# Encoder trunk: the first loads in another order, the first norms between the projections, the keys normed together

## The chip, the cores and the metric

The kernel runs on one core of a Trainium2 chip. The metric is the time of one execution on the device, in microseconds (us). Three runs of the kernel before took 3086.29, 3086.44 and 3088.57 us, median 3086.44.

## The reference, cut to what matters

The reference is an encoder trunk of two layers on 512 tokens of width 1024. What bears on the change is its beginning and the projection of the keys and values:

```python
h = layer_norm(x, ln_in_g, ln_in_b)
for l in range(DEPTH):
    proj = h @ w_in[l]
    qa, ka, va, qb, kb, vb = jnp.split(proj, SPLITS, axis=-1)
    ...
    qa = apply_axial_rope(rms_norm(qa, qn_g[l]), cos, sin)
    ka = apply_axial_rope(rms_norm(ka, kn_g[l]), cos, sin)
    oa = global_attention(qa, ka, va)
    ob = window_sink_attention(qb, kb, vb, sink[l], slopes)
    ...
```

`layer_norm` subtracts the mean of a row, divides by its standard deviation and applies a gain and a bias. `rms_norm` divides each head of 64 numbers by its root mean square. `apply_axial_rope` rotates the halves of each head by tables of cosines and sines. Behind that come attention, an output projection, another layer norm, a product-key expert layer (PEER) and a third layer norm; the change doesn't touch them.

## The kernel before, in words

The 512 tokens are four chunks of 128 rows. The tile `h` holds them with the tokens on the partitions. A float32 product is made exact enough by splitting both factors into a rounded part and a rest (`hi`, `lo`), both in a shorter matmul format, and adding three products.

The head of the kernel goes as follows.

1. SP, whose queue issues the loads, loads chunk 0 of `x` into `h` (line 144), the gain and the bias of the first layer norm (each as a copy on all 128 partitions, line 97), the chunks 1 to 3 of `x`, the identity matrix for transposes on TensorE (`ident`, line 149), and then small tables: `iota4`, `look`, `cos`, `sin`, `dist`, the gains `gq` and `gk`, `sk`, `gn`.
2. In each layer `load_split` (line 208) loads 1 MB of `w_in` into a ring of four tiles (`ws`, tag `wst`, line 138) and makes the rounded part on ScalarE (ACT, line 216) and the rest on VectorE (DVE, line 217). The first two are `w_k` and `w_v`, the keys and values of both head groups. Four of `w_q` follow.
3. A loop over the chunks 0, 1, 2, 3 (line 237) norms the chunk (layer 0 only, `layer_norm`, lines 106 to 120), transposes it by eight TensorE transposes (`transpose_rows`, line 129, with a cast on ACT in line 134 and the rest on DVE in line 136), and then multiplies it with `w_k` and with `w_v` (`proj`, lines 227 to 229, 24 matmuls each). The keys of global attention are normed and rotated at once, chunk by chunk (`norm_rope`, lines 183 to 198).
4. Then come the four blocks of `w_q` with all chunks (line 264). In the second of these the queries are normed and rotated by `norm_rope`, in the third and fourth the keys are transposed (`flip_k`).

A layer norm takes on DVE two `bn_stats` (line 110), one `bn_aggr` (line 103), an inverse square root by eleven small instructions, each of which needs the one before (`rsqrt`, lines 87 to 92), and two passes over 1024 columns (lines 114 and 116). `norm_rope` takes a square on ACT (line 188), a sum on DVE (line 189), the same `rsqrt`, three multiplications and two additions (lines 191 to 198).

The order on each engine is not the order of the source. A planner goes through the instructions with costs of its own and gives an engine the first in the source that is ready by its reckoning; the hardware then keeps that order on each engine. Tiles of one tag are a ring of so many buffers. `rsqrt` has rings of two (`rs_a`, `rs_t`) and four (`rs_y`), in which the inverse roots of the layer norms and of the key norms stand one behind the other in the order of the source.

Of the kernel before, what the change touches and what calls it, by code (L numbers as in the profile page):

```python
# [18 lines left out]
P = 128  # L19
# [26 lines left out]
def encoder_kernel(ctx: ExitStack, tc: tile.TileContext, x, ln_in_g, ln_in_b, w_in, qn_g, kn_g, sink,  # L46
# [48 lines left out]
    def bload(src, n, tag):  # L95
        t = sm.tile([P, n], F32, tag=tag, name=tag, bufs=1)
        nc.sync.dma_start(t, src[None, :].to_broadcast([P, n]))
        return t
# [41 lines left out]
        nc.sync.dma_start(t, src)  # L140
        return t

    for c in range(NC):
        nc.sync.dma_start(h[:, c, :], x[c * P:(c + 1) * P, :])
        if c == 0:
            g_in = bload(ln_in_g, D, "ln_g")
            b_in = bload(ln_in_b, D, "ln_b")
    ident = cp.tile([P, P], F32, name="ident")
    nc.sync.dma_start(ident, ident_c)
    iota4 = ws.tile([P, 2048], F32, tag="wst", name="iota4").bitcast(F16)[:, :P * 4]  # L150
    nc.sync.dma_start(iota4, iota4_c)
    iota2 = cp.tile([P, P, 2], F16, name="iota2")
# [9 lines left out]
    for l in range(L):  # L162
# [14 lines left out]
        def rotary_tables(g_t):  # L177
            for fn, src in (("c", cos), ("s", sin)):
                t = pj.tile([P, NC, HD], F32, tag="tab" + fn, name="tab" + fn, bufs=1)
                pool.tensor_tensor(out=t, in0=src, in1=bc(g_t[:, None, :], [P, NC, HD]), op=MUL)  # L180
                tabs[fn] = t

        def norm_rope(src, n, c, dst):

            nr = pj.tile([P, 3, 8, HD], F32, tag="nr", name="nr", bufs=1)
            sq, xn, t2 = (nr[:, i, :n, :] for i in range(3))
            ms = sm.tile([P, 8], F32, tag="nr_ms", name="nr_ms")[:, :n]
            act.activation(sq, src, AF.Square)
            v.tensor_reduce(out=ms, in_=sq, axis=AX.X, op=ADD)
            r = rsqrt(ms, 1.0 / HD, RMS_EPS, n, "nr")  # L190
            v.tensor_tensor(out=xn, in0=src, in1=bc(r[:, :, None], [P, n, HD]), op=MUL)
            v.tensor_tensor(out=t2, in0=xn, in1=bc(tabs["s"][:, c:c + 1, :], [P, n, HD]), op=MUL)
            v.tensor_tensor(out=xn, in0=xn, in1=bc(tabs["c"][:, c:c + 1, :], [P, n, HD]), op=MUL)
            xr = xn.rearrange("p n (a f) -> p (n a) f", a=2)
            tr = t2.rearrange("p n (a f) -> p (n a) f", a=2)
            dr_ = dst.rearrange("p n (a f) -> p (n a) f", a=2)
            v.tensor_tensor(out=dr_[:, :, :16], in0=xr[:, :, :16], in1=tr[:, :, 16:], op=ADD)
            v.tensor_tensor(out=dr_[:, :, 16:], in0=xr[:, :, 16:], in1=tr[:, :, :16], op=ADD)
# [6 lines left out]
        pj = sbuf(f"pj{l}", bufs=2)  # L205
        hTh = pj.tile([P, KD, S], F32R, name="hTh", bufs=1)
        hTl = pj.tile([P, KD, S], F32R, name="hTl", bufs=1)
        def load_split(src, nm):

            w = load_w(src, nm)  # L210
            r = []
            for i in range(2):
                x_ = w[:, i * D:(i + 1) * D]
# [16 lines left out]
            return b  # L230

        rotary_tables(gk)
        krs = {}
        if l == 0:
            layer_norm(gat[0], g_in, b_in)
        wk = load_split(w_in[l, 0], "w_k")
        for c in gat + dense:
            if l == 0 and c != gat[0]:
                layer_norm(c, g_in, b_in)
            cs = slice(c * P, (c + 1) * P)  # L240
            transpose_rows(h[:, c, :], hTh[:, :, cs], f"tr_h{c}", lo=hTl[:, :, cs])
            if c == gat[0]:
                wv = load_split(w_in[l, 1], "w_v")
            b = proj(c, wk, "ps_k")
            krs[c] = kr = pj.tile([P, 4, HD], F32, tag="kr", name="kr", bufs=NC)
            act.copy(kr.rearrange("p a d -> p (a d)"), b[:, :256])
            norm_rope(kr[:, 0:2, :], 2, c, kr[:, 0:2, :])
            b = proj(c, wv, "ps_v")
            act.copy(vN[:, c, :], b[:, :256])

        def flip_k(c):
            kh = pj.tile([P, 4, 2, HD], F32R, tag="kh", name="kh", bufs=1)
            kl = pj.tile([P, 4, 2, HD], F32R, tag="kl", name="kl", bufs=1)
            kx = bc(krs[c][:, :, None, :], [P, 4, 2, HD])
            act.copy(kh, kx)
            v.tensor_tensor(out=kl, in0=kx, in1=kh.bitcast(F32), op=SUB)
            for src, dst in ((kh, khh), (kl, kll)):
# [840 lines left out]
```

## Time and profile before

| what | value |
|---|---|
| time of the profiled execution | 3086.3 us |
| its span | 3084.5 us |
| lowest, median, highest of three runs | 3086.29, 3086.44, 3088.57 us |
| TensorE matmul (PE) busy | 2989.5 us, 97% of the span, 17858 instructions |
| TensorE weight load (PEld) busy | 2704.7 us, 88% |
| VectorE (DVE) busy | 2453.0 us, 80% |
| ScalarE (ACT) busy | 1311.1 us, 43% |
| GpSimd (POOL) busy | 748.8 us, 24% |
| granted TensorE clock, mean | 0.993 of full speed |

The busy time of an engine is the time in which it ran an instruction; idle time is told by what ended it. The first of forty equal slices of the span has PE at six tenths, all others but the second layer's beginning at eight or nine tenths. A granted clock of 1.00 is 2.4 GHz, 0.50 is 1.2 GHz; a stretch with a value between had both.

### The profile page before, as it was taken

What the parts mean: (1) busy time and instruction counts of PE and PEld (TensorE: products, weight loads), DVE (VectorE), ACT (ScalarE), POOL (GpSimd) and SP (SyncE); (2) the same over time, 40 slices, a digit from 0 to 9 for tenths busy, and PEclk for the clock granted to TensorE, in tenths of its full rate; (3) what the DMA queues carried; (4) which work ended last, traced back from release to release, by engine and by line L of the source; (5) the groups of instructions that cost most, each with busy time, mean ns of one, the idle gap of its engine ahead of it and who ended that gap; (6) DMA issues with size and microseconds to landing.
All of it is one profiled execution on the core that took longest, in us unless ns stands there. A gap on an engine that the chain in (4) does not pass through costs nothing. (4 is left out here: it accounts for less than half of the span.)

```text
span 3084.5 us, 47606 instructions
## 1 busy us (share of the span) xinstructions
PE 2989.5 (97%) x17858; PEld 2704.7 (88%) x17858; DVE 2453.0 (80%) x5207; ACT 1311.1 (43%) x2586; POOL 748.8 (24%) x524
## 2 busy tenths in 40 slices
PE   6999899999999999999999999999999999999998
PEld 6989887899999999999888888779999999999997
DVE  6777999678777777877777779987787787787777
ACT  2664268343333333333347532773433333333332
POOL 0000000014444444444000000000244344444540
PEclk9999999999999999999999999999999999999999
DMA  4113567659888888888520236675698988888882
GB/s 178 42 56 129 212 232 287 219 199 333 317 322 313 320 318 313 320 317 314 189 96 15 71 132 244 245 290 179 246 334 305 325 315 313 322 317 311 324 311 92
DMA packets 262232, 749.46 MB, mean 243 GB/s; under 512 B 19952, under 2 KB 130288, under 8 KB 231792
## 3 DMA queue, kind: packets, MB, share of 16 engines
q1 hardware_dynamic: 188272, 477.94, 42.8%
q0 software_dynamic: 73728, 268.47, 24.1%
q8 instruction: 140, 2.29, 0.3%
q14 instruction: 92, 0.75, 0.1%
HBM read 691.81 MB, written 54.53 MB: 242 GB/s over the span
## 5 line engine op out<-in xcount | busy, mean ns | idle before, releaser
L921 POOL DMA_INDIRECT gt<-in_dram,idx x512 | 742.3, 1450 | 2062.7 <-DVE idx L912 1197.7
L779 PE MATMUL ps_a<-xTh,uh 128*128 128x384 f32 x1824 | 610.6, 335 | 3.7 <-ACT uh L776 3.7
L781 PE MATMUL ps_a<-xTh,ul 128*128 128x384 f32 x1824 | 612.2, 336 | 0.0
L780 PE MATMUL ps_a<-xTl,uh 128*128 128x384 f32 x1824 | 610.8, 335 | 0.0
L966 PE MATMUL ff<-vh,wl 128*128 128x512 f32 x1476 | 576.4, 391 | 0.0
L964 PE MATMUL ff<-vh,wh 128*128 128x512 f32 x1476 | 574.9, 389 | 0.0
L965 PE MATMUL ff<-vl,wh 128*128 128x512 f32 x1476 | 574.5, 389 | 0.0
L997 ACT CAST vh<-vt 128x1024 fp32r<-128x1024 f32 x246 | 258.5, 1052 | 607.8 <-PE ff L966 308.1
L998 DVE TENSOR_TENSOR vl<-vt,vh 128x1024 fp32r<-128x1024 f32 x246 | 301.2, 1224 | 195.8 <-ACT vh L997 194.7
L779 PEld LDWEIGHTS ps_a<-xTh,uh 128*128 128x128 f32 x1824 | 342.7, 188 | 14.4 <-ACT uh L776 5.6
L780 PEld LDWEIGHTS ps_a<-xTl,uh 128*128 128x128 f32 x1824 | 342.6, 188 | 10.4
L927 DVE CUSTOM_DVE_ANT_0 junk<-gt,h 128x1024 bf16<-128x1024 f32 x256 | 313.1, 1223 | 37.6 <-DMA gt<-in_dram,idx 33.0
L781 PEld LDWEIGHTS ps_a<-xTh,ul 128*128 128x128 f32 x1824 | 342.5, 188 | 0.1
L1004 ACT CAST wh<-w 128x384 fp32r<-128x384 f32 x246 | 126.3, 513 | 478.3 <-DVE w L1001 474.3
L938 DVE SCALAR_TENSOR_TENSOR gacc<-gt,gw,gacc 128x1024 f32<-128x1024 f32 x252 | 311.6, 1280 | 21.3 <-DMA gt<-in_dram,idx 21.3
L966 PEld LDWEIGHTS ff<-vh,wl 128*128 128x128 f32 x1476 | 277.2, 188 | 57.6
L964 PEld LDWEIGHTS ff<-vh,wh 128*128 128x128 f32 x1476 | 277.0, 188 | 49.6 <-ACT wh L1004 0.9
L965 PEld LDWEIGHTS ff<-vl,wh 128*128 128x128 f32 x1476 | 277.2, 188 | 48.6
L777 DVE TENSOR_TENSOR ul<-ut,uh 128x1024 fp32r<-128x1024 f32 x228 | 277.9, 1219 | 21.7 <-ACT uh L776 21.7
L776 ACT CAST uh<-ut 128x1024 fp32r<-128x1024 f32 x228 | 239.7, 1052 | 121.8 <-PE ps_a L780 120.5
L1005 DVE TENSOR_TENSOR wl<-w,wh 128x384 fp32r<-128x384 f32 x246 | 137.5, 559 | 158.9 <-ACT wh L1004 158.9
L772 PE MATMUL ps_a<-xTd,ut 128*128 128x384 f32 x448 | 156.1, 493 | 0.0
(261 smaller groups left out, 4857.4 us busy)
## 6 DMA issues: line engine op xcount, KB each, us to landing
ut<-in_dram SPq DMA_DIRECT2D x128, 1024.0 KB, 8.4
vt<-in_dram SPq DMA_DIRECT2D x128, 1024.0 KB, 7.2
w_pq<-in_dram SPq DMA_DIRECT2D x48, 1024.0 KB, 5.0
gg<-G SPq DMA_DIRECT2D x62, 768.0 KB, 13.8
G<-stg SPq DMA_DIRECT2D x24, 1920.0 KB, 7.0
w_o<-in_dram SPq DMA_DIRECT2D x24, 1024.0 KB, 4.8
w_q<-in_dram SPq DMA_DIRECT2D x8, 1024.0 KB, 6.3
gt<-in_dram,idx POOLq DMA_INDIRECT x512, 7.3
```

Source lines behind the costliest of these rows:

```text
L777: v.tensor_tensor(out=ul.rearrange(ff), in0=us, in1=uh.rearrange(ff).bitcast(F32), op=SUB)
L779: pe.matmul(b[:, :ND], uh[:, k, :], xTh[:, k, :], start=k == 0, stop=False)
L780: pe.matmul(b[:, :ND], uh[:, k, :], xTl[:, k, :], start=False, stop=False)
L781: pe.matmul(b[:, :ND], ul[:, k, :], xTh[:, k, :], start=False, stop=k == KD - 1)
L921: pool.indirect_dma_start(out=t, out_offset=None, in_=src, in_offset=bass.IndirectOffsetOnAxis(ap=idx[:, j:j + 1], axis=0))
L927: v.tensor_tensor_reduce(out=jk, in0=t, in1=h[:, c, :], op0=MUL, op1=ADD, scale=1.0, scalar=0.0, accum_out=a_[:, j:j + 1])
L938: v.scalar_tensor_tensor(acc[j % 2], t, w_[:, j:j + 1], acc[j % 2], op0=MUL, op1=ADD)
L964: pe.matmul(b, wh[:, cs], vh[:, ns], start=blk == 0, stop=False)
L965: pe.matmul(b, wh[:, cs], vl[:, ns], start=False, stop=False)
L966: pe.matmul(b, wl[:, cs], vh[:, ns], start=False, stop=blk == NB - 1)
L997: act.copy(vh, vt[:, bi, :])
L998: v.tensor_tensor(out=vl, in0=vt[:, bi, :], in1=vh.bitcast(F32), op=SUB)
```

## The change

The loads come in another order: chunk 0 of `x`, gain, bias, `ident`, chunk 1, `w_k`, chunk 2, `w_v`, chunk 3, and only then the tables. `w_k` and `w_v` of layer 0 are loaded there and handed to `load_split`, so that nothing else is loaded for them later.

Chunk 0 is normed as before. The chunks 1 to 3 have a norm of their own, `first_norm`: ACT sums the row (a copy with a sum), DVE makes the mean and its negative from it by two small instructions, ACT sums the squares of the row less its mean, and DVE does `rsqrt` and the two passes. What ACT writes beside the sums goes into a tile of the ring `wst`. The norm of chunk c+1 stands in the source between the transposes of chunk c and its projections.

`w_k` is split behind the transposes of chunk 0, in both layers. The keys of the four chunks lie in one tile; in the loop only their squares and sums are left, and `norm_keys` does one `rsqrt` over 8 columns, three multiplications over 512 columns and eight additions for all four chunks behind the loop, in both layers.

```diff
-    for c in range(NC):
+    def load_x(c):
         nc.sync.dma_start(h[:, c, :], x[c * P:(c + 1) * P, :])
-        if c == 0:
-            g_in = bload(ln_in_g, D, "ln_g")
-            b_in = bload(ln_in_b, D, "ln_b")
+
+    load_x(0)
+    g_in = bload(ln_in_g, D, "ln_g")
+    b_in = bload(ln_in_b, D, "ln_b")
     ident = cp.tile([P, P], F32, name="ident")
     nc.sync.dma_start(ident, ident_c)
+    load_x(1)
+    w_first = [load_w(w_in[0, 0], "w_k")]
+    load_x(2)
+    w_first.append(load_w(w_in[0, 1], "w_v"))
+    load_x(3)
+
+    def first_norm(c):
+
+        hc = h[:, c, :]
+        jk = ws.tile([P, 2048], F32, tag="wst", name="sq")[:, :D]
+        s1 = sm.tile([P, 2], F32, tag="fn_s", name="fn_s")
+        mean = sm.tile([P, 2], F32, tag="fn_m", name="fn_m")
+        act.activation(jk, hc, AF.Copy, accum_out=s1[:, 0:1])
+        v.tensor_scalar(mean[:, 0:1], s1[:, 0:1], -1.0 / D, None, op0=MUL)
+        v.tensor_scalar(mean[:, 1:2], s1[:, 0:1], 1.0 / D, None, op0=MUL)
+        act.activation(jk, hc, AF.Square, bias=mean[:, 0:1], accum_out=s1[:, 1:2])
+        r = rsqrt(s1[:, 1:2], 1.0 / D, LN_EPS, 1, "fnr")
+        v.scalar_tensor_tensor(hc, hc, mean[:, 1:2], g_in, op0=SUB, op1=MUL)
+        v.scalar_tensor_tensor(hc, hc, r, b_in, op0=MUL, op1=ADD)
+
+    layer_norm(0, g_in, b_in)
...
+        def norm_keys(kr, ms):
+
+            nr = pj.tile([P, 3, 8, HD], F32, tag="nr", name="nr", bufs=1)
+            xn, t2 = (nr[:, i].rearrange("p (c n) d -> p c n d", c=NC) for i in (1, 2))
+            s4 = [P, NC, 2, HD]
+            r = rsqrt(ms.rearrange("p c n -> p (c n)"), 1.0 / HD, RMS_EPS, NC * 2, "nk").rearrange("p (c n) -> p c n", n=2)
+            v.tensor_tensor(out=xn, in0=kr[:, :, 0:2, :], in1=bc(r[:, :, :, None], s4), op=MUL)
+            v.tensor_tensor(out=t2, in0=xn, in1=bc(tabs["s"][:, :, None, :], s4), op=MUL)
+            v.tensor_tensor(out=xn, in0=xn, in1=bc(tabs["c"][:, :, None, :], s4), op=MUL)
+            for c in range(NC):
+                xr, tr, dr_ = (t[:, c, 0:2, :].rearrange("p n (a f) -> p (n a) f", a=2) for t in (xn, t2, kr))
+                v.tensor_tensor(out=dr_[:, :, :16], in0=xr[:, :, :16], in1=tr[:, :, 16:], op=ADD)
+                v.tensor_tensor(out=dr_[:, :, 16:], in0=xr[:, :, 16:], in1=tr[:, :, :16], op=ADD)
...
-        def load_split(src, nm):
-
-            w = load_w(src, nm)
+        def load_split(src, nm, w=None):
+
+            w = load_w(src, nm) if w is None else w
...
         rotary_tables(gk)
-        krs = {}
-        if l == 0:
-            layer_norm(gat[0], g_in, b_in)
-        wk = load_split(w_in[l, 0], "w_k")
+        kr = pj.tile([P, NC, 4, HD], F32, tag="kr", name="kr", bufs=1)
+        kms = sm.tile([P, NC, 2], F32, tag="k_ms", name="k_ms", bufs=1)
+        wk = wv = None
         for c in gat + dense:
-            if l == 0 and c != gat[0]:
-                layer_norm(c, g_in, b_in)
             cs = slice(c * P, (c + 1) * P)
             transpose_rows(h[:, c, :], hTh[:, :, cs], f"tr_h{c}", lo=hTl[:, :, cs])
             if c == gat[0]:
-                wv = load_split(w_in[l, 1], "w_v")
+                wk = load_split(w_in[l, 0], "w_k", w_first[0] if l == 0 else None)
+            if l == 0 and c != dense[-1]:
+                first_norm(c + 1)
+            if c == gat[0]:
+                wv = load_split(w_in[l, 1], "w_v", w_first[1] if l == 0 else None)
             b = proj(c, wk, "ps_k")
-            krs[c] = kr = pj.tile([P, 4, HD], F32, tag="kr", name="kr", bufs=NC)
-            act.copy(kr.rearrange("p a d -> p (a d)"), b[:, :256])
-            norm_rope(kr[:, 0:2, :], 2, c, kr[:, 0:2, :])
+            act.copy(kr[:, c].rearrange("p a d -> p (a d)"), b[:, :256])
+            sq = pj.tile([P, 3, 8, HD], F32, tag="nr", name="nr", bufs=1)[:, 0, :2, :]
+            act.activation(sq, kr[:, c, 0:2, :], AF.Square)
+            v.tensor_reduce(out=kms[:, c, :], in_=sq, axis=AX.X, op=ADD)
             b = proj(c, wv, "ps_v")
             act.copy(vN[:, c, :], b[:, :256])
+        norm_keys(kr, kms)
```

## Rows read from the trace of the kernel before

**Rows 1.** The view by stretches: for each stretch (us) its length, the busy time of each engine with its instructions, the granted clock, the share and the rate of the DMA engines.

```profile
0.00:60.00 60.00, 31.86 (x203) 29.72 (x204) 38.32 (x131) 14.58 (x24) 2.13 (x6) 0.94 0.52 192
60.00:280.00 220.00, 210.41 (x1656) 201.22 (x1656) 162.59 (x461) 126.46 (x434) 1.48 (x2) 0.99 0.20 72
```

**Rows 2.** The view of waits, TensorE matmuls alone, the first 62 us: who waited for whom, us in total, times, longest.

```profile
PE tr_h L129 <- DVE ln_mv L103: 12.5, 1, 12.5
PE tr_h L129 <- DVE h L116: 7.5, 3, 3.1
PE ps_k L227 <- ACT whi L216: 7.2, 1, 7.2
PE ps_k L228 <- DVE wlo L217: 0.7, 1, 0.7
```

**Rows 3.** The timeline of SP, which issues the loads: start (us), time of the issue, load.

```profile
0.75 0.39 SPq L144 DMA_DIRECT2D h<-in_dram  x1
...
3.86 0.45 SPq L149 DMA_DIRECT2D ident<-in_dram  x1
...
7.87 0.33 SPq L160 DMA_DIRECT2D sin<-in_dram  x1
9.64 0.33 SPq L161 DMA_DIRECT2D dist<-in_dram  x1
...
12.21 0.33 SPq L97 DMA_DIRECT2D gk<-in_dram  x1
...
14.09 0.50 SPq L140 DMA_DIRECT2D w_k<-in_dram  x1
...
15.11 11.75 SPq L140 DMA_DIRECT2D w_q<-in_dram  x4
```

**Rows 4.** The view of DMA issues, first 20 us: load, count, KB each, median us from issue to landing.

```profile
w_k<-in_dram SPq DMA_DIRECT2D x1, 1024.0 KB, 6.5
...
ident<-in_dram SPq DMA_DIRECT2D x1, 64.0 KB, 8.5
...
gq<-in_dram SPq DMA_DIRECT2D x1, 32.0 KB, 3.2
```

**Rows 5.** The view of waits of SP, up to 140 us: who waited for whom, us in total, times, longest.

```profile
SPq L161 <- DMA h<-in_dram: 1.4, 1, 1.4
```

**Rows 6.** The timeline of VectorE: start (us), duration, line, operation.

```profile
7.59 0.16 DVE L90 SCALAR_TENSOR_TENSOR lnrt<-lnry 128x1 f32<-128x1 f32 x1
...
9.34 1.28 DVE L116 SCALAR_TENSOR_TENSOR h<-h,lnry,ln_b 128x1024 f32<-128x1024 f32 x1
...
12.33 0.19 DVE L103 BATCH_NORM_AGGREGATE ln_mv<-ln_st 128x2 f32<-128x12 f32 x1
...
28.84 0.17 DVE L87 TENSOR_SCALAR nra<-nr_ms 128x2 f32<-128x2 f32 x1
28.92 0.15 DVE L87 TENSOR_SCALAR lnra<-ln_mv 128x1 f32<-128x1 f32 x1
...
32.39 1.28 DVE L116 SCALAR_TENSOR_TENSOR h<-h,lnry,ln_b 128x1024 f32<-128x1024 f32 x1
```

**Rows 7.** The timeline of TensorE matmuls: start (us), duration, line, operation, and in brackets the idle time before it and what ended it.

```profile
21.67 0.58 PE L227 MATMUL ps_k<-whi,hTh 128*128 128x256 f32 x1 [7.21 <-ACT whi L216]
...
33.73 1.92 PE L129 MATMUL tr_h<-ident,h 128*128 128x128 f32 x8 [3.12 <-DVE h L116]
...
62.46 0.28 PE L229 MATMUL ps_v<-whi,hTl 128*128 128x256 f32 x1
```

**Rows 8.** The view by stretches (columns as in the first group), one for each chunk: from its first projection (chunk 0) or its first transpose (chunks 1 to 3) to its last projection.

```profile
21.67:30.61 8.94, 8.26 (x48) 7.76 (x48) 6.76 (x13) 3.58 (x5) 0.00 (x0) 1.00 1.01 426
33.73:42.26 8.53, 8.52 (x56) 8.10 (x56) 4.01 (x23) 1.85 (x4) 0.00 (x0) 0.80 0.13 43
44.44:52.03 7.59, 7.35 (x56) 6.72 (x56) 4.50 (x24) 2.27 (x5) 0.00 (x0) 1.00 0.00 0
54.21:62.47 8.26, 8.26 (x56) 8.04 (x57) 4.39 (x8) 4.55 (x7) 0.00 (x0) 0.79 0.17 65
```

**Rows 9.** The view by lines, shapes apart, first 100 us (the row of L363 from the whole span): line, engine, operation, tiles and shapes, count, busy us, mean ns of one, idle us before and its releasers.

```profile
L136 DVE TENSOR_TENSOR hTl<-tr_h,hTh 128x512 fp32r<-128x512 f32 x8 | 5.3, 688 | 2.5 <-ACT hTh L134 2.5
L110 DVE BATCH_NORM_STATS2 ln_st<-h 128x6 f32<-128x512 f32 x8 | 5.1, 673 | 4.6 <-DMA h<-in_dram 4.6
...
L191 DVE TENSOR_TENSOR nr<-q,nry 128x512 f32<-128x512 f32 x3 | 2.1, 692 | 0.1
...
L198 DVE TENSOR_TENSOR kr<-nr 128x64 f32<-128x64 f32 x4 | 1.4, 358 | 0.0
...
L134 ACT CAST hTh<-tr_h 128x512 fp32r<-128x512 f32 x8 | 4.6, 586 | 21.6 <-PE tr_h L129 21.6
...
L216 ACT CAST whi<-w_k 128x1024 fp32r<-128x1024 f32 x2 | 2.0, 1042 | 5.5 <-DMA w_k<-in_dram 5.5
...
L363 ACT ACTIVATION_READ_ACCUMULATOR osq<-ps_o 128x1 f32 x128 | 26.8, 209 | 0.0
```

**Rows 10.** The view of waits, TensorE matmuls alone, from 1530 to 1590 us, the same loop in layer 1.

```profile
PE ps_k L229 <- DVE hTl L136: 2.8, 3, 1.9
PE ps_k L228 <- DVE wlo L217: 1.0, 1, 1.0
PE ps_k L227 <- ACT hTh L134: 1.0, 3, 0.4
```

More of the change, by code (lines that the diff above doesn't have):

```diff
@@ L253, in flip_k @@
             kl = pj.tile([P, 4, 2, HD], F32R, tag="kl", name="kl", bufs=1)
-            kx = bc(krs[c][:, :, None, :], [P, 4, 2, HD])
+            kx = bc(kr[:, c, :, None, :], [P, 4, 2, HD])
             act.copy(kh, kx)
```

## The prediction

> **What bounds the kernel now.** I read the busy shares first, then the slices and the stretches, then TensorE's waits in the stretch that stands out. TensorE is busy for 2989.5 of 3084.5 us, so only its 95 us of idle time and its stretches at the lower clock can be won. The slices put the largest hole at the start: in the first 60 us TensorE is busy for 31.86 us, 28.1 us idle, while the next 220 us hold 9.6 us of idle time [rows 1]. The change works in that hole. Its waits name three causes: 12.5 us until the first transpose, 7.2 us until the first key projection, and 7.5 us in three pieces before the transposes of chunks 1 to 3 [rows 2].
>
> First piece. Chunk 0 is normed at 9.34 + 1.28 = 10.62 us [rows 6], yet the transposes start at 12.5. The releaser named there had long been done; what landed then is `ident`, issued at 3.86 and 8.5 us on its way, that is 12.36 us [rows 3, 4], behind three chunks of `x`.
>
> Second piece. `w_k` is issued only at 14.09 and lands 6.5 us later at 20.6 [rows 3, 4]; the cast follows, and the first projection runs at 21.67 [rows 7].
>
> Third piece. The mean of chunk 1 is ready on VectorE at 12.33, but its inverse root begins at 28.92, directly behind the first instruction of the key root of chunk 0 at 28.84 [rows 6]. The rings of `rsqrt` are handed out in the order of the source, in which that key root stands first, and it needs the finished key projection. So each norm ends behind the projections of the chunk before (chunk 1: 32.39 + 1.28 = 33.67), and TensorE, which stops at 30.61, waits [rows 7, 8].
>
> From 54.21 on TensorE is dense, and the first query projection follows the last value projection at 62.46 without a gap [rows 7, 8]. That moment is my mark: what it moves forward should move the end forward, since all behind it is counted from compute and no later load is near its limit there.
>
> **The change, part by part.**
>
> *Loads.* `dist`, the twelfth load, waited for a chunk of `x` [rows 5]: SP issues a load when the one eight places before it has landed. So the issues of the twelfth and the fourteenth, 9.64 and 12.21 [rows 3], are the landings of chunks 1 and 3, and 512 KB take (12.21 - 9.64) / 2 = 1.28 us. The eleventh, `sin`, went at 7.87 [rows 3], the landing of the bias. In the new order: `ident` lands at about 8.0 (64 KB behind the bias), chunk 1 at 9.8, `w_k` (1 MB) at 9.8 + 2.57 = 12.4, chunk 2 at 13.7, `w_v` at 16.2, chunk 3 at 17.5. The tables follow; `cos`, `sin`, `gk` now serve only `norm_keys` behind the loop, so their delay costs nothing. The transposes start at 10.65 instead of 12.5.
>
> *ScalarE up to the first projection.* One pass of the moments is 128x1024, like the cast at 1.04, and reading the sum adds 0.21 [rows 9]: 1.25 us. Copy of chunk 1: 9.8 to 11.05; two small VectorE instructions, each needed by the next step, 0.35 (nine of that kind took 9.34 - 7.59 = 1.75 us, 0.195 each [rows 6]); Square 11.4 to 12.65. The casts of chunk 0 (ready at 11.6, when half of 1.92 us of transposes is done [rows 7]) take 2 x 0.59 [rows 9], to 13.85; the first half of `w_k` 1.04, to 14.9. So the first key projection starts at 14.9 instead of 21.67. Lower bound 13.3, if the `w_k` cast starts when it lands; upper bound 16.2 if the planner puts a pass of chunk 2 ahead too. I take 14.9, since each step is a measured duration in source order.
>
> A rule of the Trainium skill speaks against these passes: the page "ScalarE: Activation LUTs", section "Rules for kernel authors", sends plain arithmetic to VectorE. Here VectorE is the fuller one, 38.32 of 60 us against 14.58 [rows 1], so the trace doesn't bear the rule out for this stretch. By that page's fixed and per-element costs the two passes would be about 1.04 and 1.13 us, an estimate; the first projection would come 0.1 us later.
>
> *The chunks.* Chunk 0 took 8.94 us from its first projection to its last [rows 8]; I keep that, so it ends at 14.9 + 8.94 = 23.8. Per later chunk VectorE has two `bn_stats` (2 x 0.67) and the `bn_aggr` (0.19) fewer, and two small instructions more (0.35): 1.2 us off. More important, a root of the next norm no longer stands behind a key root, so norm c+1 can run beside the projections of c. VectorE's share per chunk is 11 x 0.195 for the root, 2 x 1.28 for the passes, 0.35, 2 x 0.69 for the rest of the transposed chunk and 0.29 for the key sum, 6.7 us in all [rows 6, 9], under the 7.59 us that TensorE needs for a chunk at the full clock (chunk 2, clock 1.00). Chunks 1 and 3 took 8.53 and 8.26 at clocks of 0.80 and 0.79, behind pauses of 3.1 and 2.2 us [rows 8]. Without pauses I take 7.8 for each of three (7.59 and 0.2 for the cast that the projection waits for); bounds 7.59 and 8.53. The mark: 23.8 + 3 x 7.8 = 47.2 instead of 62.46. Gain 15.2 us.
>
> *`norm_keys`.* From the last key sum: 11 small instructions (2.1 us), 3 multiplications of the size of a query's (3 x 0.69), 8 additions of 0.22 to 0.36 [rows 9]: 6 to 7 us on VectorE, against some 5 for the last chunk alone before. It lies beside the query projections, and the keys are first wanted in the third block of `w_q`, two blocks later: the 48 matmuls of a chunk take some 6 of the 7.59 us [rows 8], so two blocks of four chunks some 4 x 6 = 24 us. Cost nothing; were that cover gone, 1 to 2 us. This holds in both layers.
>
> *Layer 1.* Its loop waits for 4.8 us in all, the longest for the rest of the transposed chunk (2.8) [rows 10]. The casts of the transposed chunk now come before those of `w_k`, and the key chains no longer sit in VectorE's way. Bounds -1 (the first matmul waits longer for `w_k`) and +4; I take +1, nearer to the lower end because the layer norms before them hold the same engine.
>
> Sum: 15.2 + 1.0 = 16.2 us. The profiled execution took 3086.3 us (its span of 3084.5 and 1.8 around it), 0.1 below the median of 3086.44. Forecast 3086.3 - 16.2 = 3070.1, say 3070.
>
> **Rivals.**
>
> *A: the norms still come one by one.* If the planner, whose times for loads and transposes are its own, places a norm's pieces behind the projections on VectorE or ScalarE, the pauses stay and only the loads gain: the stretch from first projection to mark keeps its 62.46 - 21.67 = 40.8 us, the mark is 14.9 + 40.8 = 55.7, gain 6.8, time 3079.5. For it: a plan has left chunk 1's root lying from 12.33 to 28.92 before [rows 6]. Against: the ring that caused the pauses no longer stands between.
>
> *B: VectorE stands before constants.* Its queue also holds the copy of `iota4` and the scaling of `gq`, now loaded last. `gq` is the fifteenth load and can go at 13.7, when chunk 2 has landed; by its own 3.2 us [rows 4], and behind `w_v` and chunk 3 at 17.5, it lands at 17 to 19.5. If its scaling is planned before the rest of `w_k`, the second projection matmul waits until about 20 instead of 15.9; the mark is 51.4, gain 11 to 12, time 3075.
>
> *C: slower.* The loads of `w_q` come behind the scratch tiles of three moments in the same ring of four. They were issued at 15.11 [rows 3]. If the last scratch tile is handed out only when chunk 2's projections are done, `w_q` comes late. A load needs 6.5 to land [rows 4], and cast and rest 2.3; from an issue after 62.46 - 8.8 = 53.7 on the first query projection is later than before. Issued at 60, it starts at 68.8, and the end is 6.3 us later: 3092.6. Against: chunk 3 lands at 17.5 and ScalarE has time for it by 30.
>
> *D: the gain is given back.* The attention behind the mark waits 9.6 us in 220 [rows 1]; a different plan there could add waits. As much again, 9.6 us, leaves a gain of 6.6 (3080); 16 us more leave nothing (3086), 20 us more end at 3090.
>
> **How the numbers follow.** Forecast 0.67, A 0.12, B 0.11, C 0.03, D 0.07 (0.05 between 3080 and 3092, 0.02 beyond). Own range of the forecast: fast end 13.3 + 8.94 + 3 x 7.59 = 45.0, gain 17.4, with 4 of layer 1 gives 3065; slow end 16.2 + 8.94 + 3 x 8.53 = 50.7, gain 11.8, less 1 gives 3075.5. To hold the time 8 times in 10 the range takes in B and A: 3064.5 to 3080. A change within 0.2% (6.2 us) can't be told from none here. Faster by more: forecast, B and most of A, 0.88; same: the rest of A and most of D, 0.07; slower: C and the rest of D, 0.05.
>
> **What would show it.** Right: first transpose near 10.7; first key projection near 14.9; no TensorE wait for line 116 or its successor over 0.5 us; the chunks 1 to 3 near 7.8 us each at a granted clock near 1.00; the first query projection near 47; the stretches behind it as long as before. A shows as pauses of 2 to 3 us before the transposes, B as VectorE idle until `gq` or `iota4` lands, C as a cast of `w_q` that waits for its load, D as longer stretches behind the mark. I would be wrong if the mark moves by 15 and the end does not.

## The result, and the profile after

The changed kernel takes 3071.93 us (median of 6 runs, 3069.93 to 3072.94), the kernel before in runs beside it 3087.51 (6 runs, 3086.23 to 3090.54). The ratio is 0.9949, with a 95% interval of 0.9937 to 0.9961. The profiled execution took 3069.93 us, with a span of 3068.2.

The page's busy times, and the view by stretches for the stretches of [rows 1]:

```profile
PE 2986.0 (97%) x17858; PEld 2702.7 (88%) x17858; DVE 2439.6 (80%) x5120; ACT 1318.1 (43%) x2598; POOL 757.7 (25%) x524
```

```profile
0.00:60.00 60.00, 43.66 (x319) 41.67 (x320) 40.28 (x107) 26.67 (x46) 4.83 (x8) 0.97 0.63 228
60.00:280.00 220.00, 210.06 (x1641) 200.24 (x1640) 165.54 (x494) 126.22 (x442) 0.00 (x0) 0.99 0.20 70
```

TensorE's work is the same, 17858 matmuls in 2986.0 us against 2989.5. In the first 60 us it is busy for 43.66 us instead of 31.86, and from there to 280 us for as long as before. Its two longest waits in the first 62 us, to set beside [rows 2]:

```profile
PE tr_h L129 <- DVE h L116: 10.7, 1, 10.7
PE tr_h L129 <- DVE fnra L87: 2.1, 1, 2.1
```

The wait for the first transpose fell from 12.5 to 10.7, that for the first key projection from 7.2 to 1.6, and of three pauses before transposes (7.5 together) one is left, of 2.1. The timeline of TensorE shows where these stand:

```profile
10.74 1.97 PE L129 MATMUL tr_h<-ident,h 128*128 128x128 f32 x8 [10.74 <-DVE h L116]
14.32 0.58 PE L263 MATMUL ps_k<-whi,hTh 128*128 128x256 f32 x1 [1.62 <-ACT whi L252]
...
25.77 1.97 PE L129 MATMUL tr_h<-ident,h 128*128 128x128 f32 x8 [2.09 <-DVE fnra L87]
```

The chunks in the view by stretches, cut as in [rows 8] (three of chunk 3's eight transposes run early, at 35.90, and stand in chunk 2's row):

```profile
14.32:23.68 9.36, 8.10 (x48) 7.40 (x48) 8.33 (x22) 8.23 (x14) 2.68 (x2) 1.00 0.80 235
25.77:34.04 8.27, 8.27 (x56) 8.05 (x57) 7.53 (x29) 1.92 (x5) 0.00 (x0) 0.80 0.99 403
34.04:41.49 7.45, 7.21 (x61) 6.97 (x60) 2.46 (x4) 2.13 (x5) 0.00 (x0) 1.00 0.27 100
41.49:48.70 7.21, 6.80 (x55) 6.37 (x54) 3.60 (x4) 4.84 (x8) 0.00 (x0) 1.00 0.01 2
```

The first query projection, the mark of the prediction, starts at 48.7. The landings stand in SP's queue. By the prediction's rule (a load is issued when the one eight places before it has landed), these issues are the landings of `ident`, chunk 1, `w_k` and chunk 3 (chunk 2 and `w_v`, by `gq` and `gk` between them, 14.15 and 16.67; ScalarE, which waited for `w_v`, goes on at 16.68):

```profile
9.14 0.33 SPq L181 DMA_DIRECT2D cos<-in_dram  x1
10.39 0.33 SPq L182 DMA_DIRECT2D sin<-in_dram  x1
12.89 0.33 SPq L183 DMA_DIRECT2D dist<-in_dram  x1
...
18.01 0.33 SPq L97 DMA_DIRECT2D sk<-in_dram  x1
```

ScalarE's timeline, and two rows of VectorE's, tell what became of the norm of chunk 1:

```profile
11.89 0.59 ACT L134 CAST hTh<-tr_h 128x512 fp32r<-128x512 f32 x1 [9.86 <-PE tr_h L129]
...
13.22 1.99 ACT L252 CAST whi<-w_k 128x1024 fp32r<-128x1024 f32 x2
15.12 1.06 ACT L163 ACTIVATE sq<-h 128x1024 f32<-128x1024 f32 x1
16.08 0.19 ACT L163 ACTIVATION_READ_ACCUMULATOR sq<-h 128x1 f32 x1
16.68 1.04 ACT L252 CAST whi<-w_v 128x1024 fp32r<-128x1024 f32 x1 [0.41 <-DMA w_v<-in_dram]
17.63 1.15 ACT L166 ACTIVATE sq<-h,fn_m 128x1024 f32<-128x1024 f32 x1
```

```profile
19.03 0.15 DVE L87 TENSOR_SCALAR fnra<-fn_s 128x1 f32<-128x1 f32 x1
...
24.43 1.28 DVE L169 SCALAR_TENSOR_TENSOR h<-h,fnry,ln_b 128x1024 f32<-128x1024 f32 x1
```

Chunk 1 was there at 10.39 and ScalarE was idle until 11.89, but the first pass over it runs at 15.12, behind both casts of `w_k`, and the second behind a cast of `w_v`. The inverse root on VectorE starts behind the second sum, at 19.03, and the last pass ends at 25.71, where the transposes begin; in between VectorE also makes a rest of `w_v` (1.70 us) and scales `gq` (0.72), both shown in the last section. The norm ends late by both engines.

Where the time went over the whole span is best seen by stages, cut at instants of TensorE's timeline: the mark; layer 1's key loop (first key projection to first query projection); the expert (PEER) stage of each layer (last `ps_g` matmul to the first transpose of layer 1, or to the end); and all the rest of the span. All values are us of one profiled execution each.

| kernel | mark | layer 1 loop | expert 0 | expert 1 | rest | span |
|---|---|---|---|---|---|---|
| before | 62.6 | 33.3 | 1010.0 | 1019.6 | 959.0 | 3084.5 |
| after | 48.7 | 29.7 | 1010.7 | 1020.4 | 958.7 | 3068.2 |
| e1_loads | 59.1 | 33.2 | 1010.0 | 1019.6 | 959.8 | 3081.7 |
| e2_keys | 55.7 | 32.2 | 1009.3 | 1018.8 | 961.3 | 3077.3 |
| e4_rings | 62.6 | 33.2 | 1010.0 | 1019.6 | 958.8 | 3084.2 |
| e9_own_tags | 55.6 | 33.2 | 1010.0 | 1019.6 | 961.9 | 3080.3 |
| e6_keys_each | 50.0 | 31.9 | 1014.7 | 1024.2 | 960.5 | 3081.3 |
| e7_consts_late | 50.2 | 29.7 | 1010.7 | 1020.4 | 958.8 | 3069.8 |
| e8_norm_ahead | 48.3 | 29.7 | 1010.7 | 1020.3 | 961.4 | 3070.4 |
| e3_dve_moments | 47.9 | 29.7 | 1009.2 | 1018.8 | 958.4 | 3064.0 |
| e11_dve_pad | 47.8 | 29.7 | 1010.7 | 1020.2 | 959.3 | 3067.7 |
| e12_after_pad | 47.9 | 31.2 | 1009.3 | 1018.8 | 961.4 | 3068.6 |
| e10_before_pad | 63.3 | 34.0 | 1014.7 | 1024.3 | 958.4 | 3094.7 |
| e5_split_ahead | 49.6 | 33.1 | 1010.7 | 1020.3 | 960.0 | 3073.7 |

From before to after: 13.9 at the mark, 3.6 in layer 1's loop, 1.5 lost in the two expert stages, 0.3 in the rest, 16.3 together. The rest varies from 958.4 to 961.9 with no order among the kernels. A good part of that is one stretch, the attention of layer 1, which took 183.9 us in the changed kernel at a granted clock of 1.00 and 187.4 in e9_own_tags at 0.97. A difference of 3 us in a span, or between two medians, is thus no effect by itself, and the stages are what tells the kernels apart.

### The profile page after: what moved, and what is told of

Read it like the earlier page. It is cut to its first block, busy times and chain, and to the rows that moved or that the text cites. A ratio compares the mean times of both kernels' runs of the same rounds, so it can differ in the third digit from the quotient of the medians.

```text
span 3068.2 us, 47535 instructions
## 1 busy us (share of the span) xinstructions
PE 2986.0 (97%) x17858; PEld 2702.7 (88%) x17858; DVE 2439.6 (80%) x5120; ACT 1318.1 (43%) x2598; POOL 757.7 (25%) x524
```

## The experiments

### Which part took the pauses away

**e1_loads**: the kernel before with the loads' new order alone.

```diff
-    for c in range(NC):
+    load_x(0)
...
+    load_x(1)
+    w_first = [load_w(w_in[0, 0], "w_k")]
+    load_x(2)
+    w_first.append(load_w(w_in[0, 1], "w_v"))
+    load_x(3)
...
+            w = load_w(src, nm) if w is None else w
```

> The kernel before with the new order of the loads alone (w_k and w_v of layer 0 loaded between the chunks of x). Theory: loads and norms are two causes that add. The first key projection comes at 14 to 15 us instead of 21.67, the pauses of 2 to 3 us before the transposes of chunks 1 to 3 stay, the first query projection comes near 55 (62.5 less 7.3), and the time is 7 us lower, about 3079. Rival, the loads were everything: the first query projection near 48.6 as in the changed kernel, the pauses gone, time about 3072.

Measured: 3083.45 us (one run), mark 59.1. TensorE's waits in the first 62 us:

```profile
PE tr_h L129 <- DVE h L116: 18.0, 4, 10.8
PE ps_v L234 <- DVE wlo L223: 1.7, 1, 1.7
```

The first key projection came at 13.6, 8.0 us earlier, but the mark only 3.5. The three pauses are all there (18.0 - 10.8 = 7.2), and two rests of weights are late besides (1.7 for `w_v`, 1.1 for `w_k`). So in this execution the earlier loads were worth less than half their own lead while the norms went one by one. Part of what is missing is the clock: the first 59.1 us have a granted clock of 0.88, the first 62.6 before have 0.95. What the loads alone are worth at the same clock was not measured.

**e2_keys**: the kernel before with all keys normed behind the loop.

```diff
-            krs[c] = kr = pj.tile([P, 4, HD], F32, tag="kr", name="kr", bufs=NC)
-            act.copy(kr.rearrange("p a d -> p (a d)"), b[:, :256])
-            norm_rope(kr[:, 0:2, :], 2, c, kr[:, 0:2, :])
+            act.copy(kr[:, c].rearrange("p a d -> p (a d)"), b[:, :256])
...
+            v.tensor_reduce(out=kms[:, c, :], in_=sq, axis=AX.X, op=ADD)
...
+        norm_keys(kr, kms)
```

> The kernel before with the keys normed and rotated at once, alone, in both layers; loads and norms as before, moments by VectorE. Theory: with the key roots out of the rings, the roots of the layer norms run as soon as the chunks are there. First key projection at 21.7 as before, pauses before chunks 1 to 3 under 1 us each, first query projection near 55 (62.5 less three pauses of 7.5 us in all, at the most), the loop of layer 1 shorter by up to 3.7, time 3086 less 7 to 10, about 3077. Rival, it is the moments on ScalarE that remove the pauses: they stay above 2 us and the first query projection comes after 60, time 3083 to 3087.

Measured: 3076.42 us (6 runs, 3075.9 to 3079.08), ratio 0.9967 (0.9954 to 0.9979); mark 55.7. No wait before the transposes of chunks 1 to 3 is left; the waits for `ident` (13.5) and for `w_k` (7.3) stay. This part alone wins 6.9 at the mark. Without the pauses the lower clock behind them is gone too: from chunk 1's transposes to the mark the granted clock is 1.00, where chunks 1 and 3 before had 0.80 and 0.79 [rows 8].

**e4_rings** and **e9_own_tags** ask what it was in the key roots that held the norms: the length of the rings, or that norms and keys share a tag.

```diff
-        a = sm.tile([P, 16], F32, tag="rs_a", name=nm + "a")[:, :n]
+        a = sm.tile([P, 16], F32, tag="rs_a", name=nm + "a", bufs=8)[:, :n]
```

(the same for `rs_y` and `rs_t`)

> The kernel before with rings of eight instead of two, four and two for the three tiles of the inverse root; nothing else. Theory: the ring order alone held the roots of the layer norms behind the key roots, so the pauses before chunks 1 to 3 fall under 1 us, the first query projection comes near 55, time about 3079. Rival, the plan or the data put them there: the pauses stay at 3.1, 2.2 and 2.2 us and the first query projection at 62.5, time 3086.

```diff
+        g = "_ln" if nm == "lnr" else ""
-        a = sm.tile([P, 16], F32, tag="rs_a", name=nm + "a")[:, :n]
+        a = sm.tile([P, 16], F32, tag="rs_a" + g, name=nm + "a")[:, :n]
```

(the same for `rs_y` and `rs_t`)

> The kernel before with tags of their own for the three tiles of the layer norm's inverse root; nothing else. The run with longer rings changed nothing, so it was not the length. Theory: tiles of one tag are handed out in the order of the source however many there are, and the tag that layer norms and key norms share is what orders them. Then the pauses before chunks 1 to 3 fall under 1 us and the first query projection comes near 55.7, as in the run with the keys at once, time about 3079. Rival, the key chains hold VectorE by their work and not by the tag: the pauses stay at 3.1, 2.2 and 2.2 us and the first query projection at 62.5, time 3086.

Measured: longer rings 3085.98 us (one run), mark 62.6; own tags 3082.09 (one run), mark 55.6. TensorE's waits with longer rings, and then with own tags:

```profile
PE tr_h L129 <- DMA ident<-in_dram: 13.2, 1, 13.2
PE tr_h L129 <- DVE h L116: 7.5, 3, 3.1
```

```profile
PE tr_h L130 <- DMA ident<-in_dram: 12.7, 1, 12.7
PE ps_k L228 <- ACT whi L217: 7.3, 1, 7.3
```

With rings of eight the 7.5 us stay to the last digit. With tags of their own they are gone, although every key is still normed chunk by chunk. So the shared tag held the norms, and not its length. That tiles of one tag are handed out in the order of the source, with eight buffers as with two, so that the later norm stood behind the earlier key, explains both runs; no run shows the handing out itself. Both rows also name `ident` as what the first transposes waited for, which the prediction had inferred from its landing.

**e6_keys_each**: the changed kernel with the keys normed chunk by chunk.

```diff
-            sq = pj.tile([P, 3, 8, HD], F32, tag="nr", name="nr", bufs=1)[:, 0, :2, :]
-            act.activation(sq, kr[:, c, 0:2, :], AF.Square)
-            v.tensor_reduce(out=kms[:, c, :], in_=sq, axis=AX.X, op=ADD)
+            norm_rope(kr[:, c, 0:2, :], 2, c, kr[:, c, 0:2, :])
...
-        norm_keys(kr, kms)
```

> The changed kernel with the keys normed and rotated chunk by chunk again, in both layers; new loads, the norm of the next chunk ahead of the projections, moments by ScalarE. Theory of the tag: the root of the norm of chunk c+1 now stands in the source ahead of the key root of chunk c, so it is free of it even so, and the first query projection of layer 0 stays within 2 us of 48.6; layer 1, which has no first norms, loses the 3.7 us that its loop won. Time about 3073 to 3076. Rival, only the keys at once make the pauses go: pauses of 2 us and more before chunks 2 and 3, first query projection after 52, time 3077 or more.

Measured: 3083.68 us (10 runs, 3082.63 to 3084.63), ratio 0.9986 (0.9976 to 0.9995); mark 50.0, layer 1's loop 31.9. With the first norms ahead of the keys in the source, the keys one by one cost at most 1.3 us at the mark (one order gave 47.9 to 49.6 in three executions, see e12_after_pad): two parts of the change each take away the same pauses. But the time is 11.8 us above the changed kernel, and 1.3 + 2.2 explain only 3.5 of it. The expert stages, whose code is the same, are 4.0 and 3.8 us longer. That is taken up below.

### What the moments on ScalarE are worth

**e7_consts_late**: the copy of `iota4`, the scaling of `gq` and the key tables moved behind the loop, out of VectorE's and GpSimd's way. **e8_norm_ahead**: that, and the next chunk's norm ahead of the chunk's transposes in the source.

```diff
-    v.tensor_copy(iota2, iota4.rearrange("p (n t) -> p n t", t=4)[:, :, 0:2])
...
-        rotary_tables(gk)
...
+        rotary_tables(gk)
         norm_keys(kr, kms)
+        if l == 0:
...
+            v.tensor_copy(iota2, iota4.rearrange("p (n t) -> p n t", t=4)[:, :, 0:2])
+        v.tensor_scalar(gq, gq, HD ** -0.5, None, op0=MUL)
```

> The changed kernel with the copy of iota4, the scaling of gq and the tables of the key rotation on GpSimd behind the loop of the chunks. Theory: in the changed kernel the rest of w_v took 1.70 us instead of 1.22 and the scaling 0.72 instead of 0.19 while GpSimd made the tables, and both stood ahead of the root of chunk 1, which ended the one pause left (2.09 us before chunk 1). Without them the pause falls by 1 to 2 us and the first query projection by 1 to 3: 45.6 to 47.6; time 3069 to 3071. Rival, the moments that come late from ScalarE hold chunk 1, and the constants only fill the gaps: the pause stays within 0.5 us of 2.1, time 3071 to 3073.

```diff
         for c in gat + dense:
             cs = slice(c * P, (c + 1) * P)
+            if l == 0 and c != dense[-1]:
+                first_norm(c + 1)
             transpose_rows(h[:, c, :], hTh[:, :, cs], f"tr_h{c}", lo=hTl[:, :, cs])
...
-            if l == 0 and c != dense[-1]:
-                first_norm(c + 1)
```

> The same with the norm of the next chunk also ahead of the transposes of the chunk in the source, so that ScalarE takes the moments of chunk 1 ahead of the casts of chunk 0 and w_k. Theory: in the changed kernel the first pass ran at 15.12, behind four casts, though chunk 1 was there at about 10.4 and ScalarE idle until 11.9. Moved ahead, the moments of chunk 1 are done by 13, the pause before chunk 1 is gone, the first key projection comes up to 2.5 us later (near 16.5), and the first query projection near 46 to 48. Rival, the later first projection takes back all of it: first query projection at 48.6 or later.

Measured: e7_consts_late 3071.5 us (4 runs, 3070.77 to 3073.25), mark 50.2; e8_norm_ahead 3071.59 (4 runs, 3070.98 to 3073.93), mark 48.3. TensorE's waits behind chunk 0's first transpose, of the one and of the other:

```profile
PE tr_h L129 <- DVE h L169: 2.5, 1, 2.5
PE ps_k L259 <- ACT whi L248: 1.6, 1, 1.6
```

```profile
PE ps_k L259 <- ACT whi L248: 3.4, 1, 3.4
PE ps_k L261 <- DVE fnrt L91: 1.4, 1, 1.4
```

With `iota4` and `gq` out of the way the pause before chunk 1 stays, at 2.5. VectorE's timeline of e7_consts_late shows why: the inverse root still starts only when the second sum has come, and a pass over chunk 2 now stands in the middle of it (the GpSimd tables run at the old place all the same).

```profile
18.51 0.15 DVE L87 TENSOR_SCALAR fnra<-fn_s 128x1 f32<-128x1 f32 x1 [0.92 <-ACT sq L166]
...
23.63 1.27 DVE L168 SCALAR_TENSOR_TENSOR h<-h,fn_m,ln_g 128x1024 f32<-128x1024 f32 x1
```

With the norm put ahead the pause is gone, and the first key projection waits 1.8 us longer for its cast instead, and a later one 1.4 for VectorE.

**e3_dve_moments**: the changed kernel with `layer_norm`, that is `bn_stats` on VectorE, in the place of `first_norm`.

```diff
-                first_norm(c + 1)
+                layer_norm(c + 1, g_in, b_in)
```

> The changed kernel with the moments of chunks 1 to 3 on VectorE again (the layer norm of chunk 0 at the place of the new norm). Theory: where the moments are taken matters little, since VectorE has idle time before 12.5 us when the chunks land: first query projection within 1.5 us of the 48.6 of the changed kernel, time 3070 to 3074. Rival, ScalarE's moments carry the gain: the mark comes 3 us or more later, time 3075 or more.

Measured: 3067.64 us (4 runs, 3065.79 to 3069.91), ratio 0.9939 (0.9923 to 0.9956); mark 47.9. The waits of TensorE, and the stretch from 10.7 to 25.8 (up to chunk 1's transposes), of this kernel; then the same stretch of the changed kernel:

```profile
PE tr_h L129 <- DVE h L116: 10.6, 1, 10.6
PE ps_k L264 <- DVE wlo L253: 2.3, 1, 2.3
```

```profile
10.70:25.80 15.10, 10.81 (x56) 9.82 (x57) 14.91 (x32) 5.74 (x8) 2.29 (x2) 1.00 0.89 322
```

```profile
10.70:25.80 15.10, 10.10 (x57) 9.00 (x57) 11.70 (x30) 12.52 (x21) 2.68 (x2) 0.99 0.88 295
```

With the moments on VectorE that engine is full, 14.91 of 15.1 us, and the rest of `w_k` comes 1.6 us later; with the moments on ScalarE that engine is the fuller one, 12.52, and chunk 1 is held for 2.1. Chunk 1's transposes start at 25.84 in the one and at 25.77 in the other. The two ways are worth the same there. What else e3_dve_moments has ahead is 0.8 at the mark and 3.1 us in the expert stages. The 0.8 is the clock of one stretch: chunk 1 took 7.38 us at a granted clock of 1.00 here, and 8.27 at 0.80 in the changed kernel.

### Where the tiles lie

Why do the expert stages, the same instructions in the same order, take from 1009.2 to 1014.7 us in layer 0? TensorE waits there in all of these kernels for 1.8 us, and the granted clock is 1.00. What differs is where the tiles lie: every small tile that a kernel adds moves all later tiles of that side of SBUF, those that the expert stage multiplies among them. Against before, they lie 32 bytes higher in e2_keys and e3_dve_moments, 160 in the changed kernel, e7_consts_late and e8_norm_ahead, 128 in e6_keys_each, 512 in e9_own_tags and 1024 in e4_rings. Three kernels add an unused tile and nothing else.

```diff
     sm = ctx.enter_context(tc.tile_pool(name="sm", bufs=2))
+    pad = sm.tile([P, 32], F32, tag="pad", name="pad", bufs=1)
+    nc.vector.memset(pad, 0.0)
```

(128 bytes as shown, in the kernel before for **e10_before_pad** and in e3_dve_moments for **e11_dve_pad**; `[P, 96]`, 384 bytes, in the changed kernel for **e12_after_pad**)

> The kernel before with an unused tile of 128 bytes per partition ahead of the small tiles, so that every later tile of that side starts 128 bytes higher, as in the kernel with the keys normed chunk by chunk (there the expert stages took 1014.7 and 1024.2 us, against 1010.0 and 1019.6 before). Theory (the places of the tiles in SBUF set the spacing of the matmuls): the two expert stages take 1014.7 and 1024.2 us here too, +4.7 and +4.6, all other stages as before, and the time is some 9.3 us above before (3096 us, ratio 1.003). Rival (that stage was longer for what that kernel does, not for where its tiles lie): 1010.0 and 1019.6 as before, same time.

> The changed kernel with the moments by VectorE, and an unused tile of 128 bytes, so that its tiles lie where those of the changed kernel lie. Theory (of the 4.3 us that the moments on VectorE won, 0.8 are won before the first query projection and 3.1 by the places of the tiles): expert stages 1010.7 and 1020.4 us as in the changed kernel instead of 1009.2 and 1018.8, the first query projection at 47.9 as without the tile, time 3070.7 to 3071.2, that is within 0.2% of the changed kernel. Rival (the moments themselves are worth 4 us): 3067.6 as without the tile.

> The changed kernel with an unused tile of 384 bytes per partition, so that its later tiles lie 544 bytes above those of before, that is 32 bytes above a whole 512. Theory (places count by their remainder, since 512 and 1024 bytes more left before as it was and 32 more took 0.8 us from each expert stage): 1009.2 and 1018.8 us in the expert stages, mark of the first query projection 48.7 as in the changed kernel, time 3.1 us less, 3068.8. Rival: expert stages stay 1010.7 and 1020.4, time 3071.9.

Measured: e10_before_pad 3096.36 us (8 runs, 3095.1 to 3100.35), ratio 1.003 (1.0019 to 1.0041), expert stages 1014.7 and 1024.3. Before took 3087.92 in these runs, so an unused tile of 128 bytes makes it some 8 us slower, and its two expert stages are 9.4 longer. The expert stage of layer 0 in the view by stretches, before and with the tile:

```profile
540.20:1550.20 1010.00, 1008.16 (x5069) 912.65 (x5067) 784.81 (x1170) 371.62 (x496) 371.89 (x258) 1.00 0.80 290
```

```profile
540.90:1555.60 1014.70, 1012.86 (x5069) 911.63 (x5067) 784.89 (x1170) 371.19 (x496) 371.48 (x258) 1.00 0.80 288
```

TensorE does the same 5069 matmuls in 4.7 us more, and it is not idle for longer (1.84 us in both). By the view by lines, the matmuls of the second product (`ff`, 738 to a line) grew from 288.2, 287.4 and 287.3 us to 290.6, 288.1 and 289.4, 5.2 together; those of the first (`ps_a`) did not. So this is the matmuls' own pace.

e11_dve_pad took 3070.46 us (4 runs, 3069.51 to 3071.78), expert stages 1010.7 and 1020.2, mark 47.8: with its tiles placed as in the changed kernel, the version with the moments on VectorE loses its 3 us and is within 0.2% of it. e12_after_pad took 3070.36 us (4 runs, 3065.44 to 3071.4). Its expert stages came out as the theory had them, 1009.3 and 1018.8, so the remainder by 512 bytes told the pace in every kernel here (a remainder by 256 would fit the same seven places). But the time fell by 1.6, not 3.1: the profiled execution gave the 3.0 us back in layer 1's loop (+1.5) and in the rest (+2.7), 0.8 less at the mark. With the moments on ScalarE its mark is 47.9, that of e3_dve_moments: chunk 1 took 7.45 us at a granted clock of 1.00. Up to the mark every engine has the order of the changed kernel, and so it has in e5_split_ahead (below), where chunk 1 took 8.68 at 0.80 and the mark came at 49.6. So one order gives marks of 47.9, 48.7 and 49.6, and smaller differences at the mark, such as 1.3 in e6_keys_each and 1.5 in e7_consts_late, are no effect by themselves. No version measured is faster than the changed kernel by more than can be told.

### Layer 1

**e5_split_ahead**: the changed kernel, with layer 1's `w_k` split ahead of the transposes as before.

```diff
-        wk = wv = None
+        wk = load_split(w_in[l, 0], "w_k") if l else None
+        wv = None
...
-            if c == gat[0]:
+            if c == gat[0] and l == 0:
                 wk = load_split(w_in[l, 0], "w_k", w_first[0] if l == 0 else None)
```

> The changed kernel with layer 1's split of w_k ahead of the transposes as in the kernel before. Theory (the two orders each win about 1.2 us of layer 1's key loop and the rest only together, since the loop ends by whatever comes last: all keys at once alone gave 32.2, the split behind the transposes alone 31.9, both 29.7, before 33.3): layer 1's loop takes 32.2 as with the keys alone, layer 0's 48.7 as changed, time some 2.5 above the changed kernel. Rival (layer 1's gain comes from the place of the other tiles and buffers of the changed kernel, not from this order): 29.7 as changed.

Measured: 3075.49 us (one run), layer 1's loop 33.1, not 32.2. TensorE's waits in this loop, in this kernel and in the changed one (before: [rows 10], 4.8 in all):

```profile
PE ps_k L265 <- DVE hTl L136: 1.9, 1, 1.9
PE ps_k L264 <- DVE wlo L253: 1.0, 1, 1.0
PE ps_k L263 <- ACT hTh L134: 1.0, 3, 0.4
```

```profile
PE ps_k L264 <- DVE wlo L253: 1.1, 1, 1.1
PE ps_k L263 <- ACT hTh L134: 1.1, 4, 0.4
PE ps_k L265 <- DVE lnra L87: 0.3, 1, 0.3
```

The waits are 3.9 here and 2.5 in the changed kernel. So the keys at once take off 0.9 (4.8 to 3.9, and e2_keys waits 3.9 too) and the order of the split another 1.4; in e6_keys_each, with the order of the split alone, the waits are 3.1, that is 1.7 off. The two gains in waits nearly add up, and the expectation that the rest came only together was wrong. What had looked like it is the clock. From the first key projection on, two us to a row, before and then changed:

```profile
1551.60:1553.60 2.00, 0.97 (x6) 0.78 (x7) 2.00 (x4) 2.00 (x3) 0.00 (x0) 1.00 0.01 4
1553.60:1555.60 2.00, 0.79 (x8) 0.55 (x6) 2.00 (x7) 1.41 (x3) 0.00 (x0) 1.00 0.26 45
1555.60:1557.60 2.00, 1.26 (x6) 1.26 (x7) 2.00 (x7) 0.00 (x0) 0.00 (x0) 0.65 0.93 356
1557.60:1559.60 2.00, 2.00 (x11) 2.00 (x11) 2.00 (x5) 0.00 (x0) 0.00 (x0) 0.50 0.79 285
1559.60:1561.60 2.00, 2.00 (x19) 2.00 (x19) 0.66 (x3) 0.68 (x2) 0.00 (x0) 1.00 0.67 223
```

```profile
1539.50:1541.50 2.00, 0.73 (x2) 0.34 (x2) 2.00 (x4) 2.00 (x3) 0.00 (x0) 1.00 0.00 0
1541.50:1543.50 2.00, 1.84 (x15) 1.84 (x16) 2.00 (x7) 1.24 (x2) 0.00 (x0) 1.00 0.00 0
```

Before, TensorE is idle for more than half of two rows, and then the granted clock falls to 0.50, that is 1.2 GHz: a full row holds 11 matmuls instead of 19 in the next. In the changed kernel one row is as idle and the clock stays at 1.00. In e5_split_ahead the dip is longer, and its whole loop has a mean clock of 0.90. In e12_after_pad, with waits of 2.5 as in the changed kernel, the dip came all the same: 31.2 us instead of 29.7, which makes its price 1.5. The five other executions with the changed loop all took 29.7.

## Why the prediction was right, and where it wasn't

The time was forecast at 3070, and the profiled execution took 3069.9. Of the 16.2 us forecast, 15.2 were to come at the mark and 1.0 in layer 1; 13.9, 3.6 and -1.5 in the expert stages came. That these end so near is luck: 1.3 too little at the mark, 2.6 too much in layer 1 and a loss that the sum didn't have cancel each other. By the medians of six runs each the gain is 15.6.

**Loads: right.** The transposes start at 10.74 (10.65 forecast). `ident`, chunk 1, `w_k`, chunk 2, `w_v` and chunk 3 landed 0.4 to 1.1 us later than worked out, and 2.50 us lie between chunk 1 and `w_k` (2.57).

**First key projection: 14.32 instead of 14.9, for the wrong reason.** The step that failed is "each step is a measured duration in source order". The planner put both casts of `w_k` ahead of the moments. That is the case of the lower bound (13.3), later by `w_k`'s landing 0.5 late and the cast of chunk 0 ahead of it (the bound's 12.4 and 1.04 make 13.4, not 13.3); and the price I left out of that case is the norm of chunk 1, which then came late.

**The chunks: the size was off by 1.5 us.** "Without pauses" held for chunks 2 and 3, not for chunk 1. The prediction added up VectorE's share for the later chunks, 6.7 us each, and kept chunk 0 at the 8.94 of before. But chunk 1's norm now runs in chunk 0's stretch, and there VectorE also makes the four rests of `w_k` and `w_v` (2.36 us for the first two, 1.23 and 1.70 for the others), and ScalarE their casts: the row of chunk 0 has them busy for 8.33 and 8.23 of 9.36 us. That term was put at nothing. Worked out as in the prediction, 14.32 + 9.36 + 2.09 + 8.27 + 7.45 + 7.21 = 48.7 against 14.9 + 8.94 + 3 x 7.8 = 47.2: the projection 0.6 earlier, chunk 0 0.4 longer, the pause 2.1, the three chunks 0.5 shorter. Chunk 1 ran behind its pause at a granted clock of 0.80, as chunks 1 and 3 had before. The cause named for the third piece, the order of the shared rings, is shown by e9_own_tags with e4_rings against it.

**The moments on ScalarE: neither gain nor loss.** I had weighed the two engines' busy shares of 60 us. What counted was the 15 us up to chunk 1, where ScalarE has the casts of two weights besides. A pass with its sum took 1.15 and 1.24 us from start to end, against 1.25 worked out. The Trainium skill's "ScalarE: Activation LUTs", "Rules for kernel authors", would have left them on VectorE. By e3_dve_moments and e11_dve_pad that is no worse and, the places of the tiles apart, no better.

**`norm_keys`: right at nothing.** From the mark to the first score matmul it takes 54.0 us before and 54.0 in e2_keys (54.3 in the changed kernel).

**Layer 1: mis-sized, 3.6 for 1.0**, inside its bounds. The waits fell by 2.3 us, since the 2.8 for the rest of the transposed chunk went almost wholly, and the clock's dip, which I hadn't priced, left with them for some 1.4 (TensorE's busy time in the loop is 28.8 before and 27.4 after). That part wasn't sure: one of six profiled executions of the changed loop had the dip.

**"The stretches behind it as long as before": wrong by 1.5**, by where the tiles lie. In e6_keys_each the same cause costs 9.3 us (4.7 and 4.6 against before), more than half of the change's gain.

**The rivals.** A (norms one by one) is left as one pause of three. B (VectorE stands before constants) didn't come: nothing waits for a load of `gq` or `iota4`, and e7_consts_late, without them in the way, is no faster. C: `w_q` was issued at 20.5, far from the 53.7 at which it would decide. D didn't come as described, since no waits were added (the rest of the span is 0.3 shorter); what is given back is the expert stages' 1.5, in which TensorE waits for 1.8 us in both kernels.

## What to carry to other kernels

Look in the order of two chains on one engine for the buffers they share: a longer ring changed nothing here, and a tag of its own did as much at the mark as a rewritten loop (55.6 and 55.7). Price a moved step by what its engine has to do in the few microseconds before the next wait, not by busy shares of the whole stage. When a kernel's time moves by a few tenths of a per cent in a stage that wasn't touched, compare the addresses of its tiles before looking for a reason in the edit.

## What the hardware showed that I had not expected

**Tiles' places set the matmuls' pace.** 128 bytes more per partition ahead of the operands lengthen 5069 matmuls from 1008.16 to 1012.86 us, 32 bytes more (e3_dve_moments) shorten the stage by 0.8, and 512 or 1024 leave it as it was (all at a granted clock of 1.00). Which pair of operands, or which access beside them, makes the difference was not tried.

**A GpSimd operation and VectorE's stretch each other.** In the changed kernel the second of GpSimd's two tables falls on VectorE's split of `w_v`. The timeline of GpSimd, and the instructions of VectorE around it:

```profile
20.93 1.72 POOL L202 TENSOR_TENSOR tabs<-sin,gk 128x256 f32<-128x256 f32 x1
...
56.09 0.73 POOL L202 TENSOR_TENSOR tabc<-cos,gq 128x256 f32<-128x256 f32 x1
```

```profile
17.75 1.23 DVE L253 TENSOR_TENSOR wlo<-w_v,whi 128x1024 fp32r<-128x1024 f32 x1 [0.96 <-ACT whi L252]
...
20.35 1.70 DVE L253 TENSOR_TENSOR wlo<-w_v,whi 128x1024 fp32r<-128x1024 f32 x1
21.98 0.72 DVE L192 TENSOR_SCALAR gq<-gq 128x64 f32<-128x64 f32 x1
```

The same subtraction takes 1.23 and then 1.70 us, and the scaling of `gq`, 0.18 in e3_dve_moments, takes 0.72; the table takes 1.72 where the same size took 0.73 later. The Trainium skill's "SBUF — State Buffer", section "SBUF: two separate sides", has these two engines take a shared pair of ports in turn, for a whole instruction each, when VectorE reads two operands from SBUF or runs in a mode that uses two ports. The rows of the subtraction and the tables agree with the first; the scaling reads one tile, and no run here shows its mode. All of it lies ahead of chunk 1's norm, which VectorE was late with. What it costs at the mark was not measured by itself: in e7_consts_late, whose source has the tables behind the loop, they run at the same place, and that subtraction takes 1.70 us again.
